# A hybrid encoder block on one core: the DMA queue written out in the plan's order, two gates by turns behind the rewriting of the input, and other durations in the planner

## The chip, the cores and the metric

The kernel runs on one core of one Trainium2 chip. The metric is the device time of one execution in microseconds. A core has TensorE (PE in the profile, its weight loads PEld), VectorE (DVE), ScalarE (ACT), GpSimd (POOL) and SyncE (SP), which here only issues DMAs. Each engine runs its own list of instructions in order; semaphores tie the lists together.

## The reference, cut to what matters

One layer of an encoder block over 512 positions of 1024 channels, float32:

```
h = rms_norm(x); p = h @ w_in        # q|k|v of a delta net, z, decays, q|k|v of attention, gates A and B
A: conv+silu on q,k,v, l2 norms, chunked gated delta rule in both directions
   (per chunk of 64 a unit lower triangular system is solved), gated norm, @ w_dn_out
B: three groups of 8 heads, windows with dilation 1, 4, 16 (keys by residue class),
   q and k normed, ALiBi, the groups weighted by their softmax denominators, @ w_attn_out
x = x + (sigmoid(gA)*yA + sigmoid(gB)*yB) @ w_o
x = x + (silu(conv(gate)) * conv(up)) @ w_ffn_down,  gate|up = rms_norm(x) @ w_ffn_up
```

## The kernel before, in words

Every dense product is made from three float32r matmuls (`mm3`, lines 317 to 320): operands are split into a high part and a rest, and high times high, high times rest and rest times high are added up in PSUM. Weights come from DRAM in blocks by class `Stream`: `load` (line 59) issues the DMA of a block into one of three buffers `wst`; `fetch` (line 69) has ScalarE write the high part `whi` (line 80) and GpSimd or VectorE the rest `wlo` (line 82); `block` hands out a block and fetches three further ones, each with two more loaded behind it.

The order of the dense work is the list `SEQ` (line 39): K (with the sum of squares of x beside it), AB (the delta net's decay and beta inputs, 32 columns), Q, then twelve attention units U (a head pair of one group each, `att_dense`, eight blocks of 384 columns), with V, Z and the sixteen gates between them, then YA, YB and WO and the feed-forward part. The units of groups 1 and 2, and all gates after unit 3, work on the input in residue-class order. So between unit 3 and the next gate the split input `hh`, `hl` is written anew: `by_classes` and `by_class` (lines 291 to 313) load x once more, scale it (line 304), let ScalarE write the high part (line 309) and VectorE the rest (line 311), for eight slices of 128 channels.

Beside the dense stream run generators: `chain` (delta net: decays, norms, gram matrices, the solve, the scan of eight chunks), `norms` and `queue` (attention: `att_norms` with the Newton iteration of `newton` at lines 257 to 262 and the transposes at 682 and 684, then `att_softmax`), and `combine` for each of four head pairs, which sends statistics through DRAM, makes weights, reads them back as broadcast tiles `alb` (line 850) and multiplies the group outputs with them (line 852). The solve is 31 steps of two VectorE operations (lines 957 and 960) on `xi`; its result goes to DRAM twice (`dx`, lines 964 and 965, the second transposed by VectorE, line 963) and comes back by twelve DMAs in other layouts (lines 973 and 976).

Where their instructions stand among the dense ones is decided by class `Driver` when the program is written: it keeps a clock `now`, advances it by each dense step (0.695 us, or 0.53 us in a unit), charges every VectorE, ScalarE and GpSimd operation a duration (`V`, `S`, `G`), and resumes a generator when its time is due. A generator that yields a number waits so long: LOAD for a DMA, TRIP for a way through DRAM and back, LATE before TensorE uses something, PACE between steps of the solve. `Slots` and `room` keep count of buffers by the planned time of their release. The line that fixes which engines keep that order is

```
ctx.enter_context(tc.manual_schedule(engines={PE, Activation, DVE, Pool}))      # names shortened
```

SP isn't in it: its DMAs are put in order by the framework's own scheduler. `drv.finish(dn)` ends the chain before the last LAST gates, and `post` (the gated norm) runs beside those.

Of the kernel before, what the change touches and what calls it, by code (L numbers as in the profile page):

```python
# [20 lines left out]
T = 512  # L21
# [12 lines left out]

UNITS = [(0, p) for p in range(4)] + [(g, p) for p in range(4) for g in (1, 2)]
GATES = [(n, d) for n in ("GA", "GB") for d in range(8)]
LAST = 4

SEQ = ([("K", 0), ("AB", 0)] + [("Q", i) for i in range(4)] + [("U", 0)] + [("V", i) for i in range(4)]
       + [("Z", 0), ("U", 1), ("Z", 1), ("Z", 2), ("U", 2), ("Z", 3), GATES[0], ("U", 3)]  # L40
       + [x for i in range(4, 12) for x in (GATES[i - 3], ("U", i))] + GATES[9:]
       + [(n, d) for n in ("YA", "YB") for d in range(8)] + [("WO", d) for d in range(8)])

LOAD, TRIP, LATE = 5.0, 9.0, 1.0
PACE = 2.0
TAIL, WARM = 2, 11
NBLK = {"K": 8, "AB": 1, "Q": 2, "V": 2, "U": 8, "Z": 2, "YB": 1, "GB": 2, "YA": 1, "GA": 2, "WO": 2}
WIDTH = {"AB": 256, "U": 384}


# [69 lines left out]
class Driver:  # L120
# [16 lines left out]
        self.end = max(self.end, t)  # L137

    def V(self, n, k=1):
        self.charge("V", k * (0.09 + n * 1.15e-3))  # L140
        return self.nc.vector

    def S(self, n, k=1):
# [72 lines left out]
def hybrid(tc, A, out):  # L216
# [3 lines left out]
    def pool(stack, name, side=None, **kw):  # L220
        kw.setdefault("reuse_waits", "tile")
        if side:
            kw["side"] = side
        return stack.enter_context(tc.tile_pool(name=name, bufs=1, **kw))

    ctx.enter_context(tc.manual_schedule(engines={mybir.EngineType.PE, mybir.EngineType.Activation, mybir.EngineType.DVE,
                                                   mybir.EngineType.Pool}))
    drv = Driver(nc)
    V, S, G, pe = drv.V, drv.S, drv.G, drv.pe
    cp = pool(ctx, "cp")  # L230
# [23 lines left out]
    def newton(y, x, tmp, scale, bias):  # L254
# [4 lines left out]
        for _ in range(3):  # L259
# [8 lines left out]
    ones = cp.tile([128, 128], F32, name="ones")  # L268
    nc.gpsimd.memset(ones, 1.0)
    ws = Stream(drv, nc, wp, A["wa"], [WIDTH.get(n, 512) for n, _ in SEQ for _ in range(NBLK[n])], 3, 6, "a",  # L270
                {b for b, n in enumerate(n for n, _ in SEQ for _ in range(NBLK[n])) if n in ("U", "Q", "V", "Z", "GA", "GB")})
    wt = Tiles(ws, 4)


# [14 lines left out]
    used = []  # L289

    def by_classes():
        xs = []
        for k in range(KD):
            while len(xs) < min(k + 2, KD):
                yield from drv.room(T2)
                xs.append(t2("xk"))
                nc.sync.dma_start(xs[-1], A["xt"][:, len(xs) - 1, :])
            while k not in used:
                yield 0.3
            drv.add(by_class(k, xs[k]))  # L300

    def by_class(k, xk):
        w = vec[:, V_N1 + k:V_N1 + k + 1]
        V(512).scalar_tensor_tensor(xk, xk, w, rstd, op0=ALU.mult, op1=ALU.mult)
        yield
        parts(k, "r")
        xo = xk.rearrange("p (j r) -> p r j", r=4)
        ho, lo = (a.rearrange("p (r j) -> p r j", r=4) for a in (hh[k], hl[k]))
        S(1024).activation(ho, xo, AF.Copy)
        yield  # L310
        V(900).tensor_tensor(lo, xo, ho.bitcast(F32), ALU.subtract)  # L311
        drv.give(T2)
        flags["class", k] = True

    acc = cp.tile([128, T], F32, name="acc", tag="rstd")

# [6 lines left out]
    warm = small_ps()  # L323
    for _ in range(WARM):
        nc.tensor.matmul(warm[:, 0:128], ones, ones, start=True, stop=True)
    for k in range(KD):
        xk = t2("xk")
        nc.sync.dma_start(xk, A["xt"][:, k, :])
        ws.fetch(min(k + 2, 8))
        hidden(k, xk)  # L330
        sq = acc if k == 0 else t2("sq")
        nc.scalar.activation(sq, xk, AF.Square)
        if k:
            nc.gpsimd.tensor_tensor(acc, acc, sq, ALU.add)
        if k == 5:
            nc.vector.tensor_copy(con[:, 0:1], xk[:, 0:1])
            nc.sync.dma_start(con, A["con"])
        wh, wl = ws.block(0)
        for m in range(4):
            c = slice(m * 128, m * 128 + 128)  # L340
            mm3(kps[m], wh[:, c], wl[:, c], hh[k], hl[k], k == 0, k == KD - 1)
# [47 lines left out]
            drv.dense(0.695)  # L389
        return ps  # L390

    def h_dense(ps=None, classes=False):
        def part(k):
            if classes:
                drv.until(lambda: ("class", k) in flags)
            return hh[k]
        return cm_dense(part, lambda k: hl[k], KD, ps)

    def conv(src, w0, scale_bc):

# [254 lines left out]
    def att_norms(u, qk):  # L655
# [9 lines left out]
        for i in range(2):  # L665
            V(512).tensor_reduce(ss[:, 0, i * 8:i * 8 + 8], sqs[i].rearrange("p i (a c) -> p i a c", c=64),  # L666
                                 axis=AX.X, op=ALU.add)
        drv.give(T2, 2)
        newton(ss[:, 1], ss[:, 0], ss[:, 2], 1.0 / 64, EPS)
        qk4 = qk.rearrange("p i (a c) -> p i a c", c=64)  # L670
        V(1024).tensor_tensor(qk4, qk4, ss[:, 1].rearrange("p (i a) -> p i a", a=4)[:, :, :, None]
                              .to_broadcast([128, 4, 4, 64]), ALU.mult)
# [127 lines left out]
    def combine(p):  # L800
# [4 lines left out]
        for g in (1, 2):  # L805
            nc.sync.dma_start(dst[p, g - 1].rearrange("(i r) c -> i (r c)", r=4),
                              stat[:, g].rearrange("p r h c -> p (r h c)"))
        for g in (1, 2):
            nc.sync.dma_start(nstat[:, g].rearrange("p a h c -> p a (h c)"),
                              dst[p, g - 1].rearrange("(a p) c -> p a c", p=128))  # L810
        V(16).tensor_copy(nstat[:, 0], stat[:, 0])
        yield TRIP
        al = ap_.tile([128, 3, 4, 2], F32, name="al")
        nM = ap_.tile([128, 4, 2], F32, name="nM")
        tt = ap_.tile([128, 4, 2], F32, name="tt")
# [26 lines left out]
        nc.sync.dma_start(o, dog[p])  # L842
        yield LOAD
        drv.give(T2)
        for g in range(3):
            yield from drv.room(T2)
            e = t2("alb")
            for h in range(2):
                c = (g * 2 + h) * 4
                nc.sync.dma_start(e[HALF[h]], daw[p, c:c + 4].rearrange("a t -> (a t)")[None].to_broadcast([64, T]))  # L850
            yield LOAD
            V(512).tensor_tensor(ogs[g, p], ogs[g, p], e, ALU.mult)
            drv.give(T2)
            if g:
                V(512).tensor_tensor(o, o, ogs[g, p], ALU.add)
# [22 lines left out]
    def gram(s):  # L878
        yield from drv.room(PG, 2)
        pg_ = [small_ps(), small_ps()]  # L880
        for p in range(4):
            for e, hf in DIAG:
                R = HALF[e]
                nc.tensor.matmul(pg_[e][HALF[hf], p * 128:p * 128 + 128], kq[R, p, s, 0, hf, :], kq[R, p, s, :, hf, :],
                                 start=True, stop=True)
        pe(2.4)
        for f in range(2):
            dg = dgs[s, f]
            for e in range(2):
                g4 = pg_[e].rearrange("p (q c t) -> p c q t", c=2, t=64)  # L890
                o4 = lambda x: x[:, f, s].rearrange("p (q e) t -> p e q t", e=2)[:, e]
                V(256).tensor_tensor(o4(cx), g4[:, 0], par(dg, e), ALU.mult)
                V(256).tensor_tensor(o4(qd), g4[:, 1], par(dg, e), ALU.mult)
                if f:
                    drv.give(PG)
            yield
            G(512).tensor_tensor(cx[:, f, s], cx[:, f, s], bc64(hs(AA, f, s)), ALU.mult)
            c = C_QKM + f * 64
            G(512).tensor_tensor(qd[:, f, s], qd[:, f, s], con[:, None, c:c + 64].to_broadcast([128, 8, 64]), ALU.mult)

    dgs = {}

# [13 lines left out]
    def chain():  # L916
# [30 lines left out]
        for f in range(2):  # L947
            for a in range(2):
                for b in range(2):
                    P = slice(a * 64 + b * 32, a * 64 + b * 32 + 32)  # L950
                    nc.sync.dma_start(du(dl)[f, a, b], cx[P, f].rearrange("p s h t -> p (s h) t")[:, :, b * 32:b * 32 + 32])
        nc.sync.dma_start(lt, dl)
        yield 2 * LOAD
        for j in range(31):
            n = 31 - j
            t4 = tmp[:, 0:2 * n * (j + 1)].rearrange("p (b i c) -> p b i c", b=2, i=n)
# [2 lines left out]
            xr = xi[:, :, j + 1:32, 0:j + 1]  # L959
            V(2 * n * (j + 1)).tensor_tensor(xr, xr, t4, ALU.add)  # L960
            yield PACE
        xt_ = n3.tile([128, 2, 32, 32], F32, name="xt_", tag="lt")
        V(2048).tensor_copy(xt_, xi.rearrange("p b i j -> p b j i"))
        nc.sync.dma_start(dx[0], xi)
        nc.sync.dma_start(dx[1], xt_)
        aux = n1.tile([128, 2, 32, 32], F32, name="aux", tag="tmp")
        cxf = cx.rearrange("p f s h t -> p f (s h) t")
        for f in range(2):
# [234 lines left out]
    def dense(n, i):  # L1203
        if n == "U":
            att_unit(i)
        elif n == "V":
            begin(qkv_tile("V", 8 + i, vT[:, i], h_dense(), PD))
        elif n == "Z":
            begin(out_gate(i, h_dense()))
        else:  # L1210
            begin(gate(GATES.index((n, i)), h_dense(None, classes), classes))

    for n, i in order[:-LAST]:
        dense(n, i)
# [100 lines left out]
    x1 = xp.tile([128, KD, T], F32, name="x1")  # L1315
    h2h = [cp.tile([128, T], F32R, name="h2h", tag=f"hh{k}") for k in range(KD)]
    h2l = [cp.tile([128, T], F32R, name="h2l", tag=f"hl{k}") for k in range(KD)]
    acc2 = xp.tile([128, T], F32, name="acc2")
    ws2 = Stream(drv, nc, xp, A["wb"], [1024] * A["wb"].shape[0], 2, 4, "b")
    for d in range(KD):  # L1320
        xk = t2("xk2")
        nc.sync.dma_start(xk, A["xt"][:, d, :])
        ps = cm_dense(lambda k: mh[:, k], lambda k: ml[:, k], KD)
        V(512).tensor_tensor(x1[:, d], ps, xk, ALU.add)
        drv.give(PD)
# [66 lines left out]
def prep(inputs):  # L1392
# [19 lines left out]
    for n, i in SEQ:  # L1412
# [4 lines left out]
        elif n == "U":  # L1417
            g, p = UNITS[i]
            c = slice((g * 8 + 2 * p) * 64, (g * 8 + 2 * p + 2) * 64)
            new = list(np.concatenate([kp(wq)[:, :, c], kp(wk)[:, :, c], kp(wv)[:, :, c]], axis=2))  # L1420
        else:
            new = rows(src[n][i])
        assert len(new) == NBLK[n]
# [61 lines left out]
```

## Time and profile before

| | |
|---|---|
| median of 3 runs | 1076.61 us (1075.24 to 1076.73) |
| the profiled execution | 1076.4 us, its span 1074.5 us |
| PE busy | 1008.2 us (94%), 6653 matmuls |
| DVE / ACT / POOL busy | 668.5 (62%) / 434.4 (40%) / 245.7 us (23%) |
| chain that ended last | PE 71%, DVE 14%, issue 5%, ACT 3%, DMA 3%, POOL 3% |
| DMA | 114.61 MB, queue of SP 33.1% of 16 engines' span |

A line of a timeline reads: start in us, duration in us, engine, line, operation, output and inputs, count, and in brackets the idle time of the engine before it and what ended it. "PEclk" is the TensorE clock that was granted, as a share of full speed.

### The profile page before, as it was taken

What the parts mean: (1) busy time and instruction counts of PE and PEld (TensorE: products, weight loads), DVE (VectorE), ACT (ScalarE), POOL (GpSimd) and SP (SyncE); (2) the same over time, 40 slices, a digit from 0 to 9 for tenths busy, and PEclk for the clock granted to TensorE, in tenths of its full rate; (3) what the DMA queues carried; (4) which work ended last, traced back from release to release, by engine and by line L of the source; (5) the groups of instructions that cost most, each with busy time, mean ns of one, the idle gap of its engine ahead of it and who ended that gap; (6) DMA issues with size and microseconds to landing.
All of it is one profiled execution on the core that took longest, in us unless ns stands there. A gap on an engine that the chain in (4) does not pass through costs nothing.

```text
span 1074.5 us, 17109 instructions
## 1 busy us (share of the span) xinstructions
PE 1008.2 (94%) x6653; PEld 841.3 (78%) x6653; DVE 668.5 (62%) x1139; ACT 434.4 (40%) x857; POOL 245.7 (23%) x229
## 2 busy tenths in 40 slices
PE   9879898987999959989999999999999999999998
PEld 7569686975999848878788787878888888888886
DVE  5384976569677634664765767667777225777621
ACT  5246445646555424334236423434334113433410
POOL 3234464523444512343443000200000000000000
PEclk9889998998999969999999999999999999999999
DMA  5222233542233482222364445412222322222331
GB/s 188 81 73 74 81 106 110 123 150 84 75 99 98 152 139 65 81 81 71 96 187 149 166 137 195 149 47 91 98 98 84 130 81 79 98 99 79 109 126 40
DMA packets 80288, 114.61 MB, mean 107 GB/s; under 512 B 32624, under 2 KB 45264, under 8 KB 79824
## 3 DMA queue, kind: packets, MB, share of 16 engines
q1 hardware_dynamic: 77328, 108.29, 33.1%
q10 hardware_dynamic: 2880, 5.24, 1.3%
q8 instruction: 52, 0.85, 0.3%
q14 instruction: 28, 0.23, 0.1%
HBM read 101.04 MB, written 12.47 MB: 106 GB/s over the span
## 4 chain that ended last, share of the span: by engine, by line
PE 71%; DVE 14%; issue 5%; ACT 3%; DMA 3%; POOL 3%; SPq 1%; POOLq 0%; ACTq 0%; DVEq 0%
PE dps L318 21%; PE dps L319 20%; PE dps L320 20%; POOL wlo L82 2%; PE gps L719 2%; PE gps L770 1%; DMA wst<-in_wa 1%; PE gps L754 1%; DMA xk<-in_xt 1%; DVE ass L666 1%; DVE wlo L82 1%; DVE cy L408 1%; PE gps L1060 1%; ACT whi L80 1%; DVE ass L260 1%
## 5 line engine op out<-in xcount | busy, mean ns | idle before, releaser
L82 POOL TENSOR_TENSOR wlo<-wst,whi 128x384 fp32r<-128x384 f32 (+1 forms) x152 | 178.9, 1186 | 322.8 <-ACT whi L80 286.8
L80 ACT ACTIVATE whi<-wst 128x384 fp32r<-128x384 f32 (+2 forms) x259 | 174.1, 690 | 129.3 <-PE dps L319 66.2
L318 PE MATMUL dps<-h2h,whi 128*128 128x512 f32 x352 | 139.2, 395 | 0.0
L320 PE MATMUL dps<-h2h,wlo 128*128 128x512 f32 x352 | 139.0, 395 | 0.0
L319 PE MATMUL dps<-h2l,whi 128*128 128x512 f32 x352 | 139.0, 395 | 0.0
L82 DVE TENSOR_TENSOR wlo<-wst,whi 128x1024 fp32r<-128x1024 f32 (+2 forms) x107 | 115.2, 1086 | 18.8 <-ACT whi L80 18.8
L406 ACT ACTIVATE cy<-pre,vec 128x512 f32<-128x512 f32 x56 | 40.6, 725 | 146.0 <-DVE pre L403 145.9
L318 PE MATMUL dps<-whi,hr 128*128 128x384 f32 x256 | 93.1, 364 | 0.0
L319 PE MATMUL dps<-wlo,hr 128*128 128x384 f32 x256 | 87.8, 343 | 0.0
L320 PE MATMUL dps<-whi,lr 128*128 128x384 f32 x256 | 87.8, 343 | 0.0
L319 PEld LDWEIGHTS dps<-h2l,whi 128*128 128x128 f32 x352 | 66.1, 188 | 16.0
L318 PEld LDWEIGHTS dps<-h2h,whi 128*128 128x128 f32 x352 | 66.1, 188 | 16.0
L320 PEld LDWEIGHTS dps<-h2h,wlo 128*128 128x128 f32 x352 | 66.1, 188 | 15.9
L318 PE MATMUL dps<-ah,whi 128*128 128x512 f32 x176 | 69.8, 397 | 0.0
L319 PE MATMUL dps<-al__7594,whi 128*128 128x512 f32 x176 | 69.6, 396 | 0.0
L320 PE MATMUL dps<-ah,wlo 128*128 128x512 f32 x176 | 69.2, 393 | 0.0
L408 DVE SCALAR_TENSOR_TENSOR cy<-pre,vec,cy 128x511 f32<-128x511 f32 x56 | 44.8, 799 | 36.2 <-ACT cy L406 36.1
L742 ACT ACTIVATE sb<-sb,stat 128x128 f32<-128x128 f32 (+1 forms) x96 | 40.8, 426 | 53.2 <-DVE stat L731 53.0
L1385 DVE TENSOR_TENSOR x<-x,dps 128x512 f32<-128x512 f32 x16 | 11.0, 686 | 78.8 <-PE dps L320 78.8
L318 PE MATMUL dps<-hh,whi 128*128 128x512 f32 x128 | 55.0, 430 | 2.1 <-ACT hh L286 2.1
L318 PE MATMUL dps<-hr,whi 128*128 128x512 f32 x120 | 50.4, 420 | 4.3 <-DVE v L646 2.4
L319 PE MATMUL dps<-lr,whi 128*128 128x512 f32 x120 | 48.9, 408 | 5.9 <-DVE lr L311 5.9
(298 smaller groups left out, 2112.8 us busy)
## 6 DMA issues: line engine op xcount, KB each, us to landing
wst<-in_wb SPq DMA_DIRECT2D x66, 512.0 KB, 3.2
wst<-in_wa SPq DMA_DIRECT2D x96, 256.0 KB, 2.7
wst<-in_wa SPq DMA_DIRECT2D x96, 192.0 KB, 2.3
xk<-in_xt SPq DMA_DIRECT2D x24, 256.0 KB, 3.3
dgt<-gt ACTq DMA_DIRECT2D x16, 256.0 KB, 2.0
alb<-daw SPq DMA_DIRECT2D x24, 128.0 KB, 3.2
dg<-dgd SPq DMA_DIRECT2D x16, 128.0 KB, 2.9
ga<-dgt SPq DMA_DIRECT2D x8, 256.0 KB, 3.8
```

The source lines that it names most:

```text
L80: self.drv.S(w).activation(hi[:, :w], st[:, :w], AF.Copy)
L82: eng(w).tensor_tensor(lo[:, :w], st[:, :w], hi[:, :w].bitcast(F32), ALU.subtract)
L260: V(n).tensor_mul(tmp, x, y)
L318: nc.tensor.matmul(ps, wh, xh, start=first, stop=False)
L319: nc.tensor.matmul(ps, wh, xl, start=False, stop=False)
L320: nc.tensor.matmul(ps, wl, xh, start=False, stop=last)
L406: S(512).activation(y, pre, AF.Copy, scale=w[1])
L408: V(512).scalar_tensor_tensor(y[:, 1:], pre[:, :-1], w[0], y[:, 1:], op0=ALU.mult, op1=ALU.add)
L666: V(512).tensor_reduce(ss[:, 0, i * 8:i * 8 + 8], sqs[i].rearrange("p i (a c) -> p i a c", c=64), axis=AX.X, op=ALU.add)
L719: nc.tensor.matmul(pss[h][:, t], qT[H, x, i:i + 128], kT[H, y, i:i + w], start=(n == 0), stop=(n == 2))
L742: S(w, 1.15).activation(sbs[b, h][:, t], sbs[b, h][:, t], AF.Exp, bias=st[:, 0:1], accum_out=st[:, 1:2])
L1385: V(512).tensor_tensor(x1[:, d], x1[:, d], ps, ALU.add)
```

## The change

SP's DMAs too stand in the order in which the program is written; so loads are written earlier (x in `load_x`, two `alb` tiles at once), and generators yield between writing to DRAM and reading back. Gates 1 and 2 become one item GP after the rewriting, whose blocks alternate, and one gate goes to the end, so that units 4 and 5, and 10 and 11, are neighbours. While slices 3 to 7 are rewritten, the solve pauses. The rewriting gets precedence (delays of -2). PACE is 1 for 2, LATE 1.5 for 1, TRIP 8 for 9, LAST 5 for 4. A VectorE operation is charged at least 0.28 us.

```diff
-LAST = 4
+LAST = 5
...
-       + [x for i in range(4, 12) for x in (GATES[i - 3], ("U", i))] + GATES[9:]
+       + [("GP", 1), ("U", 4), ("U", 5)] + [x for i in range(6, 11) for x in (GATES[i - 3], ("U", i))] + [("U", 11)]
+       + GATES[8:]
...
-LOAD, TRIP, LATE = 5.0, 9.0, 1.0
-PACE = 2.0
+LOAD, TRIP, LATE = 5.0, 8.0, 1.5
+PACE = 1.0
...
     def V(self, n, k=1):
-        self.charge("V", k * (0.09 + n * 1.15e-3))
+        self.charge("V", k * max(0.28, 0.08 + n * 1.2e-3))
...
-    ctx.enter_context(tc.manual_schedule(engines={mybir.EngineType.PE, mybir.EngineType.Activation, mybir.EngineType.DVE,
-                                                   mybir.EngineType.Pool}))
+    ctx.enter_context(tc.manual_schedule())
...
-            drv.add(by_class(k, xs[k]))
+            drv.add(by_class(k, xr[k]), -2.0)
...
         flags["class", k] = True
+        if k == 2:
+            flags["rewrite"] = True
+        if k == KD - 1:
+            del flags["rewrite"]
...
+    def load_x(upto):
+        while len(xs) < min(upto, KD):
+            xs.append(t2("xk"))
+            nc.sync.dma_start(xs[-1], A["xt"][:, len(xs) - 1, :])
+
+    load_x(1)
+    ws.load(1)
+    load_x(2)
     for k in range(KD):
-        xk = t2("xk")
-        nc.sync.dma_start(xk, A["xt"][:, k, :])
+        xk = xs[k]
         ws.fetch(min(k + 2, 8))
+        load_x(k + 3)
...
+        if k == KD - 1:
+            ws.fetch(9)
...
+    def pair_dense():
+        drv.need(PD, 2)
+        ps = [dense_ps(), dense_ps()]
+        for k0 in (0, 4):
+            for i in range(2):
+                wh, wl = ws.block()
+                for k in range(k0, k0 + 4):
+                    drv.until(lambda: ("class", k) in flags)
+                    c = slice((k - k0) * 128, (k - k0) * 128 + 128)
+                    mm3(ps[i], wh[:, c], wl[:, c], hh[k], hl[k], k == 0, k == KD - 1)
+                    drv.dense(0.695)
+        return ps
...
         drv.give(T2, 2)
+        yield
         newton(ss[:, 1], ss[:, 0], ss[:, 2], 1.0 / 64, EPS)
+        yield
...
+        yield LOAD
         for g in (1, 2):
             nc.sync.dma_start(nstat[:, g].rearrange("p a h c -> p a (h c)"),
...
-        yield TRIP
+        yield LOAD
...
+        es = []
         for g in range(3):
-            yield from drv.room(T2)
-            e = t2("alb")
...
+            while len(es) < min(g + 2, 3):
+                yield from drv.room(T2)
+                e = t2("alb")
...
+                es.append((e, drv.now + LOAD))
+            yield max(0.0, es[g][1] - drv.now)
...
             yield PACE
+            while "rewrite" in flags:
+                yield 0.5
         xt_ = n3.tile([128, 2, 32, 32], F32, name="xt_", tag="lt")
+        nc.sync.dma_start(dx[0], xi)
         V(2048).tensor_copy(xt_, xi.rearrange("p b i j -> p b j i"))
-        nc.sync.dma_start(dx[0], xi)
+        yield
         nc.sync.dma_start(dx[1], xt_)
+        yield TRIP
```

The two GpSimd masks after a gram matrix become a generator of their own, and the loads of x beside WO go one step further ahead, by `load_x`.

## Rows read from the trace of the kernel before

**Rows 1.** Busy time by stretch: stretch, its length, engines (instructions), PEclk, DMA share, GB/s.
```profile
0.00:600.00 600.00, 539.64 (x4641) 465.31 (x4641) 388.25 (x770) 275.10 (x640) 235.90 (x222) 0.95 0.37 107
600.00:1050.00 450.00, 447.69 (x1924) 359.51 (x1925) 277.49 (x367) 159.28 (x218) 9.79 (x7) 1.00 0.33 110
```
**Rows 2.** Who PE waited for: us in total, times, longest.
```profile
PE gps L682 <- DVE qk L671: 21.8, 4, 12.5
PE dps L319 <- DVE lr L311: 5.9, 2, 5.5
PE gps L505 <- DVE pre L499: 4.7, 1, 4.7
...
PE dps L318 <- DVE v L646: 2.4, 1, 2.4
...
PE gps L320 <- DVE wlo L82: 2.3, 1, 2.3
```
**Rows 3.** Busy time in the K steps and behind five of the waits; columns as in rows 1.
```profile
7.00:33.30 26.30, 24.93 (x99) 19.45 (x99) 13.82 (x16) 13.56 (x24) 10.81 (x9) 0.94 0.48 148
...
36.84:46.00 9.16, 9.16 (x30) 4.48 (x31) 0.62 (x2) 1.26 (x2) 2.51 (x2) 0.67 0.45 143
59.64:67.00 7.36, 7.36 (x28) 5.87 (x29) 4.34 (x10) 3.06 (x10) 1.28 (x1) 0.54 0.02 3
178.70:183.30 4.60, 4.58 (x16) 4.01 (x17) 2.51 (x4) 3.23 (x6) 1.07 (x2) 0.56 0.17 61
...
264.90:271.40 6.50, 6.11 (x17) 5.00 (x18) 1.94 (x3) 1.61 (x2) 1.07 (x2) 0.50 0.11 42
...
397.35:404.80 7.45, 7.45 (x105) 6.62 (x107) 3.27 (x5) 2.28 (x4) 1.01 (x1) 0.51 0.12 18
```
**Rows 4.** Timeline of PE: two of the four waits at line 682.
```profile
178.72 1.11 PE L682 MATMUL gps<-con,qk 128*128 128x128 f32 x4 [5.25 <-DVE qk L671]
220.21 1.06 PE L682 MATMUL gps<-con,qk 128*128 128x128 f32 x4 [2.64 <-DVE qk L671]
```
**Rows 5.** Timeline of DVE: one Newton iteration beside GpSimd, one without, the last rewritten slice.
```profile
170.36 0.59 DVE L257 TENSOR_SCALAR ass<-ass 128x16 f32<-128x16 f32 x1
...
177.43 1.23 DVE L671 TENSOR_TENSOR qk<-qk,ass 128x1024 f32<-128x1024 f32 x1
...
260.32 0.17 DVE L257 TENSOR_SCALAR ass<-ass 128x16 f32<-128x16 f32 x1
...
262.63 1.23 DVE L671 TENSOR_TENSOR qk<-qk,ass 128x1024 f32<-128x1024 f32 x1
...
265.80 1.07 DVE L311 TENSOR_TENSOR lr<-xk,hr 128x512 fp32r<-128x512 f32 x1
```
**Rows 6.** Timeline of POOL: one of six operations in a row, 169 to 176 us.
```profile
173.10 1.05 POOL L897 TENSOR_TENSOR cx<-cx,sm 128x512 f32<-128x512 f32 x1
```
**Rows 7.** Line 957, a solve step's first operation: ns min/median/max, first and last start.
```profile
L957 DVE TENSOR_TENSOR tmp<-lt,xi x31: 224/608/1626, 230.7 to 365.2; 128x62 f32<-128x62 f32 x2, 128x120 f32<-128x120 f32 x2, 128x174 f32<-128x174 f32 x2, 128x224 f32<-128x224 f32 x2
```
**Rows 8.** Timeline of SP's queue behind the solve.
```profile
370.13 0.41 SPq L965 DMA_DIRECT2D dx<-xt__3767  x1
371.82 0.34 SPq L976 DMA_DIRECT2D aux<-dx  x1
377.15 2.15 SPq L973 DMA_DIRECT2D cx<-dx  x4
...
385.55 1.21 SPq L66 DMA_DIRECT2D wst<-in_wa  x2
386.82 1.09 SPq L850 DMA_DIRECT2D alb<-daw  x2
```
**Rows 9.** Who waited for whom from 366 to 400 us.
```profile
ACT whi L80 <- DMA wst<-in_wa: 19.4, 3, 13.0
DVE og L852 <- DMA alb<-daw: 14.4, 1, 14.4
```
**Rows 10.** DMA issues by line: count, KB each, us from issue to landing.
```profile
alb<-daw SPq DMA_DIRECT2D x24, 128.0 KB, 3.2
```

More of the change, by code (lines that the diff above doesn't have):

```diff
@@ L36 @@
 GATES = [(n, d) for n in ("GA", "GB") for d in range(8)]
-LAST = 4
+LAST = 5
 SEQ = ([("K", 0), ("AB", 0)] + [("Q", i) for i in range(4)] + [("U", 0)] + [("V", i) for i in range(4)]
        + [("Z", 0), ("U", 1), ("Z", 1), ("Z", 2), ("U", 2), ("Z", 3), GATES[0], ("U", 3)]
-       + [x for i in range(4, 12) for x in (GATES[i - 3], ("U", i))] + GATES[9:]
+       + [("GP", 1), ("U", 4), ("U", 5)] + [x for i in range(6, 11) for x in (GATES[i - 3], ("U", i))] + [("U", 11)]
+       + GATES[8:]
        + [(n, d) for n in ("YA", "YB") for d in range(8)] + [("WO", d) for d in range(8)])
-LOAD, TRIP, LATE = 5.0, 9.0, 1.0
-PACE = 2.0
+LOAD, TRIP, LATE = 5.0, 8.0, 1.5
+PACE = 1.0
 TAIL, WARM = 2, 11
-NBLK = {"K": 8, "AB": 1, "Q": 2, "V": 2, "U": 8, "Z": 2, "YB": 1, "GB": 2, "YA": 1, "GA": 2, "WO": 2}
+NBLK = {"K": 8, "AB": 1, "Q": 2, "V": 2, "U": 8, "Z": 2, "YB": 1, "GB": 2, "GP": 4, "YA": 1, "GA": 2, "WO": 2}
 WIDTH = {"AB": 256, "U": 384}
@@ L270, in hybrid @@
     ws = Stream(drv, nc, wp, A["wa"], [WIDTH.get(n, 512) for n, _ in SEQ for _ in range(NBLK[n])], 3, 6, "a",
-                {b for b, n in enumerate(n for n, _ in SEQ for _ in range(NBLK[n])) if n in ("U", "Q", "V", "Z", "GA", "GB")})
+                {b for b, n in enumerate(n for n, _ in SEQ for _ in range(NBLK[n])) if n in ("U", "Q", "V", "Z", "GA", "GB", "GP")})
     wt = Tiles(ws, 4)
@@ L291, in by_classes @@
     def by_classes():
-        xs = []
+        xr = []
         for k in range(KD):
-            while len(xs) < min(k + 2, KD):
+            while len(xr) < min(k + 2, KD):
                 yield from drv.room(T2)
-                xs.append(t2("xk"))
-                nc.sync.dma_start(xs[-1], A["xt"][:, len(xs) - 1, :])
+                xr.append(t2("xk"))
+                nc.sync.dma_start(xr[-1], A["xt"][:, len(xr) - 1, :])
             while k not in used:
                 yield 0.3
-            drv.add(by_class(k, xs[k]))
+            drv.add(by_class(k, xr[k]), -2.0)
     def by_class(k, xk):
@@ L304, in by_class @@
         V(512).scalar_tensor_tensor(xk, xk, w, rstd, op0=ALU.mult, op1=ALU.mult)
-        yield
+        yield -2.0
         parts(k, "r")
@@ L309, in by_class @@
         S(1024).activation(ho, xo, AF.Copy)
-        yield
+        yield -2.0
         V(900).tensor_tensor(lo, xo, ho.bitcast(F32), ALU.subtract)
@@ L325, in hybrid @@
         nc.tensor.matmul(warm[:, 0:128], ones, ones, start=True, stop=True)
+    xs = []
+    def load_x(upto):
[5 more added lines that the diff above has]
+    load_x(2)
     for k in range(KD):
-        xk = t2("xk")
-        nc.sync.dma_start(xk, A["xt"][:, k, :])
+        xk = xs[k]
         ws.fetch(min(k + 2, 8))
+        load_x(k + 3)
         hidden(k, xk)
@@ L390, in cm_dense, with h_dense @@
         return ps
[L392 to L397, printed above, removed]
+    def h_dense(ps=None):
+        return cm_dense(lambda k: hh[k], lambda k: hl[k], KD, ps)
+    def pair_dense():
[10 more added lines that the diff above has]
+        return ps
     def conv(src, w0, scale_bc):
@@ L844, in combine @@
         drv.give(T2)
+        es = []
         for g in range(3):
-            yield from drv.room(T2)
-            e = t2("alb")
[L848 to L852, printed above, removed]
+            while len(es) < min(g + 2, 3):
+                yield from drv.room(T2)
+                e = t2("alb")
+                for h in range(2):
+                    c = (len(es) * 2 + h) * 4
+                    nc.sync.dma_start(e[HALF[h]], daw[p, c:c + 4].rearrange("a t -> (a t)")[None].to_broadcast([64, T]))
+                es.append((e, drv.now + LOAD))
+            yield max(0.0, es[g][1] - drv.now)
+            V(512).tensor_tensor(ogs[g, p], ogs[g, p], es[g][0], ALU.mult)
             drv.give(T2)
@@ L896, in gram, with masks @@
             yield
-            G(512).tensor_tensor(cx[:, f, s], cx[:, f, s], bc64(hs(AA, f, s)), ALU.mult)
-            c = C_QKM + f * 64
-            G(512).tensor_tensor(qd[:, f, s], qd[:, f, s], con[:, None, c:c + 64].to_broadcast([128, 8, 64]), ALU.mult)
+            drv.add(masks(f, s))
+    def masks(f, s):
+        G(512).tensor_tensor(cx[:, f, s], cx[:, f, s], bc64(hs(AA, f, s)), ALU.mult)
+        c = C_QKM + f * 64
+        G(512).tensor_tensor(qd[:, f, s], qd[:, f, s], con[:, None, c:c + 64].to_broadcast([128, 8, 64]), ALU.mult)
+        yield
     dgs = {}
@@ L951, in chain @@
                     nc.sync.dma_start(du(dl)[f, a, b], cx[P, f].rearrange("p s h t -> p (s h) t")[:, :, b * 32:b * 32 + 32])
+        yield LOAD
         nc.sync.dma_start(lt, dl)
-        yield 2 * LOAD
+        yield LOAD
         for j in range(31):
@@ L961, in chain @@
             yield PACE
+            while "rewrite" in flags:
+                yield 0.5
         xt_ = n3.tile([128, 2, 32, 32], F32, name="xt_", tag="lt")
+        nc.sync.dma_start(dx[0], xi)
         V(2048).tensor_copy(xt_, xi.rearrange("p b i j -> p b j i"))
-        nc.sync.dma_start(dx[0], xi)
+        yield
         nc.sync.dma_start(dx[1], xt_)
+        yield TRIP
         aux = n1.tile([128, 2, 32, 32], F32, name="aux", tag="tmp")
@@ L1207, in dense @@
             begin(qkv_tile("V", 8 + i, vT[:, i], h_dense(), PD))
+        elif n == "GP":
+            for j, ps in enumerate(pair_dense()):
+                begin(gate(i + j, ps, True))
         elif n == "Z":
@@ L1210, in dense @@
         else:
-            begin(gate(GATES.index((n, i)), h_dense(None, classes), classes))
+            begin(gate(GATES.index((n, i)), h_dense(), classes))
     for n, i in order[:-LAST]:
@@ L1317, in hybrid @@
     h2l = [cp.tile([128, T], F32R, name="h2l", tag=f"hl{k}") for k in range(KD)]
+    xs.clear()
     acc2 = xp.tile([128, T], F32, name="acc2")
@@ L1320, in hybrid @@
     for d in range(KD):
-        xk = t2("xk2")
-        nc.sync.dma_start(xk, A["xt"][:, d, :])
+        load_x(d + 2)
+        xk = xs[d]
         ps = cm_dense(lambda k: mh[:, k], lambda k: ml[:, k], KD)
@@ L1420, in prep @@
             new = list(np.concatenate([kp(wq)[:, :, c], kp(wk)[:, :, c], kp(wv)[:, :, c]], axis=2))
+        elif n == "GP":
+            a, b = (rows(src[m][j]) for m, j in GATES[i:i + 2])
+            new = [a[0], b[0], a[1], b[1]]
         else:
```

## The prediction, on record before the changed kernel ran

> **What bounds the kernel now.** I read first the busy time in two long stretches [rows 1]. From 600 to 1050 us TensorE is busy for 447.69 of 450 us at full clock: 1924 matmuls, 0.2327 us each. Nothing in the diff shortens a matmul there, so all that can be won lies before 600 us. There TensorE is busy for 539.64 of 600 us, at a mean clock of 0.95. So 60 us are idle, and about 0.05 x 540 = 27 us go to the lower clock.
>
> Next comes the list of what TensorE waited for [rows 2]; the reader is to see that nearly all of its long waits end on VectorE, and that one line, the transposes behind the attention norms, holds 21.8 us in four waits, one of them 12.5 us. Third, the stretches behind those waits [rows 3]: behind each the granted clock is lower (0.50 to 0.67 as a mean: mostly the lower of its two levels, 1.2 GHz). A wait here costs its length and then (1 - clock) x busy. Fourth, SP's queue at the longest wait [rows 8, 9].
>
> **The change part by part.** Durations are those of the profiled execution, 1076.4 us in all (span 1074.5), 0.2 us below the median of the runs shown.
>
> *K steps and AB.* The split of the AB block (its rest on VectorE) now stands ahead of the last K products, not behind the Newton iteration that waits for them. The 2.3 us wait [rows 2] goes, and with it the slow stretch: 0.33 x 9.16 = 3.0 us [rows 3]. The eight K steps take 26.3 us, of which 96 matmuls x 0.2327 = 22.3 are work; x two slices ahead could give back up to 4.0 us, but weights and x still share one queue in turns and four buffers, so I take 1. Sum 6.3, bounds 0 and 9.3.
>
> *Decays (line 505).* 4.7 us, and 0.46 x 7.36 = 3.4 us of clock behind it [rows 2, 3]. Sixteen operations of 64 elements were charged 0.09 + 64 x 0.00115 = 0.164 us and are now charged 0.28: 16 x 0.116 = 1.9 us, and LATE adds 0.5. So 2.4 us more dense work stands ahead of the waiting matmuls. The rest of the wait stays, and I leave the clock with it. Gain 2.4, bounds -1 (placed later than needed, the chain's successors come later) and 8.1.
>
> *Attention norms (line 682).* Without the 12.5 us wait the three others make 21.8 - 12.5 = 9.3 us, 5.25 and 2.64 among them [rows 2, 4], hence a third of 1.4. Eleven operations of 16 elements go from 0.108 to 0.28 us in the plan: 1.9, with LATE 2.4 us. Each wait shrinks by at most that: 1.4 + 2.4 + 2.4 = 6.2. Clock behind the 5.25 us: 0.44 x 4.58 = 2.0, not counted. Bounds: all of it, 11.3, and -3, if the later transposes hold back the softmax and so the next unit.
>
> That charge is where a rule weighs against the change. The same eleven operations took 262.63 - 260.32 = 2.3 us in one place and 177.43 - 170.36 = 7.1 us in another [rows 5], where GpSimd ran operations of about 1 us one behind the other [rows 6]. The charge of 11 x 0.28 = 3.1 us covers the first and not the second. The Trainium skill, page SBUF — State Buffer, section "Who interferes with whom", says that a VectorE operation with two SBUF inputs and a GpSimd operation that reads SBUF exclude each other for the whole of the one that began first. The stretched operations agree with it; by it a charge per operation can't be right for both places, which is the second rival below.
>
> *Rewriting (line 311).* The gate behind unit 3 waited 5.9 us for the rest of slices 6 and 7, then 0.5 x 6.11 = 3.1 us went to the clock [rows 2, 3]. The last slice was written at 265.80 us, behind the norms of unit 3 (to 263.9) and solve steps [rows 5]. Now both stand back: the solve pauses, the rewriting has precedence, and TensorE has two gates' products on slices 0 to 3 (8 x 0.695 = 5.6 us, before 2.8) before it needs slice 4. That is 2.8 us of cover more, and VectorE freed of 3.5 us of norms (Newton and the scaling, 260.32 to 263.9). 6.3 us exceed 5.9. I take 7.5 of 9.0, since unit 3's norms now come later; bounds 0 and 9.
>
> *Behind the solve.* SP issued the second write at 370.13 and the first read back at 371.82, then stood until 377.15 for the write to land; the twelve reads took until 385.55, and only then came weights and `alb` [rows 8]. ScalarE waited 13.0 us for weights, VectorE 14.4 us for `alb` with the norms of a unit queued behind that multiplication [rows 9]; TensorE's waits of 2.4 and 12.46 us followed, then 0.49 x 7.45 = 3.7 us of clock: 18.6 us [rows 2, 3]. In plan order eight planned microseconds lie between write and reads, in which weights and `alb` are issued. The standing (5.3 us) goes; the issuing of twelve (8.4 us) stays, with weights behind it, but six blocks of 12 x 0.175 = 2.1 us are ahead (0.175: 0.2327 x 384/512, an estimate), 12.6 us of cover against 8.4 plus a landing. I take 12, since something of `alb` may still fall behind the twelve; bounds 0 and 18.6. If the cover is gone, the wait is back.
>
> *What it adds.* A queue written in plan order stops at every DMA whose data isn't there; weights are behind it then. No row shows that order. Bounds: a little below nothing, since the other stalls before 600 us could also shrink (say 2 us), and on the other side one or two waits as behind the solve, 12.46 + 3.7 = 16.2 us each. I take half of one, 8. PACE 1: the solve took 136 us for 31 steps, 4.4 each [rows 7]; one microsecond less each brings the scan some 25 us forward, but VectorE's work gets denser there. Units 4 and 5 as neighbours: the fourth PSUM bank of unit 4 waits for two gate evictions; with the denser VectorE 0.8 us. LAST, the masks, the three yields elsewhere and `load_x` beside WO: nothing; dense work with its weights ahead hides them, as the full stretch after 600 us shows [rows 1], and what they would cost without it is inside the 8 us.
>
> Sum: 6.3 + 2.4 + 6.2 + 7.5 + 12 - 8 - 0.8 = 25.6 us; 1076.4 - 25.6 = **1051 us**.
>
> **The rivals.**
> - *The wait behind the solve moves.* With PACE 1 the solve's end meets the combination of the first head pair elsewhere, and `alb` or weights again stand behind the twelve reads. For it: the 8.4 us are unchanged, and the plan charges SP nothing for issuing. Against: the standing before them is gone. No gain of 12: 1063 us.
> - *VectorE becomes the bound.* Where GpSimd splits weights beside the norms, eleven operations cost 7.1 us against 3.1 charged, and the denser solve takes VectorE's gaps. The 2.4 and 6.2 are lost, and a wait of 5.25 us comes twice more: 1051 + 8.6 + 10.5 = 1070 us. By the rule of the skill named above this comes wherever the two meet.
> - *Given back.* The order of the queue was good already, and the holes only wander: 1076 us, no change.
> - *Slower: each combination stalls.* `alb` lands 3.2 us after issue [rows 10] and is planned at LOAD = 5. If SP is over 1.8 us behind the plan at the issue, because a weight load ahead waits for GpSimd, VectorE stops at line 852 with the norms behind it. Before, one of four combinations did this, for 14.4 us; if the three others do too, each with 16.2 us: 1076.4 - 22.4 + 48.6 = 1103 us (no gain behind the solve). At half of that the whole gain is gone. Against it: twelve such multiplications, and only one waited, in a queue that also waits for GpSimd.
>
> **How the numbers follow.** The forecast 0.52 (its own range 1038 to 1060), the moved wait 0.20, VectorE 0.12, given back 0.06, slower 0.10. From 1035 to 1074 us about two in ten are left out: the last two cases and a small part below. A measurement here tells changes of over 0.2%, 2.2 us, from none. Faster: 0.52 + 0.20 + 0.11 = 0.83; same 0.06; slower 0.11.
>
> **What would show it.** Right: no wait of TensorE over 4 us between 30 and 600 us except perhaps near line 505; the clock at 1.00 where the rewriting ends and behind the solve; weights issued between the writes and the reads of `dx`; the solve over in about 110 us. Wrong: ScalarE waiting over 10 us for weights, VectorE over 5 us for `alb`, or a busy share of TensorE before 600 us no higher than now.

## The result, and the profile after

The changed kernel takes 1045.07 us (median; before, on the same chip, 1075.92): a ratio of 0.9718, 95% interval 0.9692 to 0.9745. That is 30.9 us less; 25.6 were forecast, 1051 us.

The page of the changed kernel: span, busy time, granted clock in 40 slices, the chain that ended last.

```profile
span 1043.2 us, 17128 instructions
...
PE 1001.0 (96%) x6653; PEld 838.3 (80%) x6653; DVE 676.1 (65%) x1139; ACT 433.3 (42%) x857; POOL 252.8 (24%) x229
...
PEclk9999989989999989999999999999999999999999
...
PE 67%; DVE 14%; issue 6%; ACT 5%; DMA 4%; POOL 2%; SPq 2%; POOLq 0%; ACTq 0%; DVEq 0%
```

Busy time by stretch, which answers to [rows 1], columns as there; the third line is the stretch from the end of unit 3 to the start of unit 4.

```profile
0.00:570.00 570.00, 537.11 (x4673) 466.77 (x4673) 401.05 (x783) 277.67 (x646) 243.19 (x222) 0.97 0.39 114
570.00:1020.00 450.00, 444.38 (x1897) 356.13 (x1898) 272.98 (x353) 155.67 (x212) 9.59 (x7) 1.00 0.32 108
...
235.90:258.00 22.10, 16.40 (x88) 12.66 (x89) 15.01 (x27) 15.28 (x32) 8.61 (x8) 0.92 0.19 58
```

TensorE idles for 33 of the first 570 us, where it idled for 60 of 600. By the mean clocks of the whole spans, 0.969 before and 0.982 after, the lower clock cost 0.031 x 1074.5 = 33 us and now costs 0.018 x 1043.2 = 19.

Who TensorE waited for, the longest of the list and the two that answer to [rows 2] (line 710 was 682, 311 kept its number):

```profile
PE dps L322 <- DVE z L1214: 5.1, 1, 5.1
PE gps L798 <- DVE pt L787: 4.4, 4, 1.7
PE dps L322 <- ACT v L677: 4.4, 1, 4.4
PE gps L782 <- ACT sb L770: 4.3, 2, 3.0
PE dps L322 <- DVE pre L429: 2.6, 1, 2.6
PE gps L531 <- DVE pre L525: 2.2, 1, 2.2
...
PE gps L710 <- DVE qk L699: 0.5, 1, 0.5
...
PE dps L323 <- DVE lr L311: 0.2, 1, 0.2
```

The 21.8 us behind the norms are 0.5, the 5.9 us behind the last slices 0.2, the 4.7 us of the decays 2.2, and the wait for the AB split is gone. In their place stand waits that were short or not there: 5.1 us of unit 1 for a PSUM bank (0.7 before), 4.3 us for exponentials (2.1 before), and 4.4 us for ScalarE's copies of unit 3 (none before), just where the rewriting is.

Where the lead arises can be read by landmarks that both programs have, from the starts and ends of their matmuls (us):

| | before | after | lead | of it in this stretch |
|---|---|---|---|---|
| unit 0 starts | 77.7 | 67.5 | 10.2 | 10.2 |
| unit 3 ends | 252.7 | 235.9 | 16.8 | 6.6 |
| unit 5 ends (gates 0 to 2 done in both) | 321.3 | 303.8 | 17.5 | 0.7 |
| unit 7 ends | 373.5 | 359.9 | 13.6 | -3.9 |
| YA starts | 607.1 | 571.7 | 35.4 | 21.8 |
| the norm of the feed-forward part starts | 702.0 | 671.1 | 30.9 | -4.5 |

SP's queue behind the solve, which answers to [rows 8]:

```profile
350.69 0.33 SPq L1002 DMA_DIRECT2D dx<-xi  x1
351.12 9.36 SPq L67 DMA_DIRECT2D wst<-in_wa  x3
360.57 0.35 SPq L869 DMA_DIRECT2D daw<-awT  x1
...
361.37 0.42 SPq L1005 DMA_DIRECT2D dx<-xt__3731  x1
361.89 1.73 SPq L67 DMA_DIRECT2D wst<-in_wa  x2
363.67 3.26 SPq L881 DMA_DIRECT2D alb<-daw  x4
...
367.61 1.46 SPq L1014 DMA_DIRECT2D cx<-dx  x2
...
379.14 2.11 SPq L67 DMA_DIRECT2D wst<-in_wa  x1
```

Weights and four of the six `alb` loads now go out between the write (361.37) and the reads (367.61). The twelve reads still hold the queue, for 11.5 us. And the second write itself is late: 10.7 us pass between the two writes, where 3.4 passed before. VectorE has the transposed copy ready at 357.7 us, and until 361.4 the write stands behind weights, whose buffers GpSimd is still reading (SP waits 8.2 us for that between the two writes), and behind the write of `daw`. GpSimd's subtraction in front of them took 3.46 us beside that copy of 2.35 us; the next one of the same size, without it, took 1.29 us.

Of the signs that the prediction gave of being right, three are missing: TensorE has two waits of over 4 us between 30 and 600 us (5.1 and 4.4), the clock is 0.92 in the stretch with the rewriting and 0.93 from 350 to 400 us, not 1.00, and the solve took 129 us, not 110. One of its signs of being wrong is there too: ScalarE waited 11.3 us for weights behind the twelve reads (until 383.3 us). TensorE had cover for it; from 360 to 400 us it waited 2.0 us for the reads themselves and 2.0 us for VectorE.

### The profile page after: what moved, and what is told of

The parts are those of the page before. It is cut to its first block, busy times and chain, and to the rows that moved or that the text cites. A ratio compares the mean times of both kernels' runs of the same rounds, so it can differ in the third digit from the quotient of the medians.

```text
span 1043.2 us, 17128 instructions
## 1 busy us (share of the span) xinstructions
PE 1001.0 (96%) x6653; PEld 838.3 (80%) x6653; DVE 676.1 (65%) x1139; ACT 433.3 (42%) x857; POOL 252.8 (24%) x229
## 4 chain that ended last, share of the span: by engine, by line
PE 67%; DVE 14%; issue 6%; ACT 5%; DMA 4%; POOL 2%; SPq 2%; POOLq 0%; ACTq 0%; DVEq 0%
PE dps L322 20%; PE dps L323 20%; PE dps L324 20%; DMA wst<-in_wa 3%; POOL wlo L83 2%; PE gps L747 1%; PE gps L798 1%; DVE wlo L83 1%; ACT sb L770 1%; DVE tmp L994 1%; ACT whi L81 1%; DVE ass L261 1%; PE gps L782 1%; DVE cy L434 1%; DVE ass L260 1%
## 5 line engine op out<-in xcount | busy, mean ns | idle before, releaser
L83 POOL TENSOR_TENSOR wlo<-wst,whi 128x384 fp32r<-128x384 f32 (+1 forms) x152 | 184.6, 1226 | 284.4 <-ACT whi L81 264.4
L83 DVE TENSOR_TENSOR wlo<-wst,whi 128x1024 fp32r<-128x1024 f32 (+2 forms) x107 | 117.6, 1106 | 20.9 <-ACT whi L81 20.8
L322 PE MATMUL dps<-whi,hh 128*128 128x384 f32 x128 | 46.7, 365 | 7.7 <-DVE z L1214 5.1
```

What stands on the lines that cost most here:

```text
L83: eng(w).tensor_tensor(lo[:, :w], st[:, :w], hi[:, :w].bitcast(F32), ALU.subtract)
L322: nc.tensor.matmul(ps, wh, xh, start=first, stop=False)
```

## The experiments

Each is the changed kernel or the kernel before with the edit shown, timed beside the kernel before. Differences in the last column are those of the ratios x 1075 us; the changed kernel is 0.9718 by that measure. A difference of two such ratios is known to 0.3 to 0.5% (3 to 5 us): the 4 us of a_no_pair can't be told from nothing, and the 4 us of a_sp_auto only just.

| | edit | us (median) | ratio, 95% interval | against changed or before |
|---|---|---|---|---|
| a_sp_auto | changed, SP by the framework | 1040.19 | 0.9679 (0.9662 to 0.9696) | -4 |
| b_sp_plan | before, SP in plan order | 1086.8 | 1.0107 (1.009 to 1.0124) | +12 |
| a_old_times | changed, old durations | 1060.22 | 0.9864 (0.9841 to 0.9887) | +16 |
| a_old_charge | changed, old VectorE charge | 1059.71 | 0.9851 (0.9808 to 0.9893) | +14 |
| a_dx_at_once | changed, no yield at dx | 1049.67 | 0.9765 (0.9751 to 0.978) | +5 |
| a_alb_dx | changed, that and alb singly | 1054.37 | 0.9812 (0.979 to 0.9833) | +10 |
| b_alb_dx | before, alb in twos, yield at dx | 1058.07 | 0.9856 (0.9824 to 0.9888) | -15 |
| a_no_pair | changed, gates singly, LAST 4 | 1047.86 | 0.9751 (0.9724 to 0.9779) | +4 |
| a_no_pause | changed, no pause, no precedence | 1032.64 | 0.9612 (0.9578 to 0.9647) | -11 |
| a_no_prec | changed, no precedence | 1056.1 | 0.983 (0.9795 to 0.9865) | +12 |
| a_pace2 | changed, PACE 2 | 1058.95 | 0.9862 (0.9827 to 0.9897) | +15 |
| a_best | changed, no pause, no precedence, SP by the framework | 1022.96 | 0.9522 (0.9489 to 0.9556) | -21 |

### The order of the queue, both ways

```diff
-    ctx.enter_context(tc.manual_schedule())                       # a_sp_auto; b_sp_plan is the reverse, in the kernel before
+    ctx.enter_context(tc.manual_schedule(engines={PE, Activation, DVE, Pool}))
```

> The changed kernel with SP's DMAs ordered by the framework again, all else as changed. Theory (plan order is what took the wait behind the solve away): that wait returns, ScalarE waits over 8 us for weights behind the read back of dx, 1045 + 10 to 18 = 1055 to 1063 us. Rival (the yields, durations and the order of units did it, the queue's order is worth nothing): 1042 to 1048 us and no such wait.

> The kernel before with one edit, SP's DMAs in program order. Theory (the order pays only with yields between a write to DRAM and its read back, as SP stands at the first read): 1066 to 1082 us, SP standing some 5 us or more at the first read of dx with weights behind it. Rival (the order alone brings most of the gain): below 1060 us.

Measured: a_sp_auto 4 us less than the changed kernel, b_sp_plan 12 us more than the kernel before. So the theory of the first is wrong, and its rival was only half right: the plan's order isn't worthless, it costs. In the second, SP stood at the first read as expected (5.2 us), but the time is above the range given for it. In a_sp_auto four `alb` loads go out at 363.89 us, ahead of nine of the twelve reads, with no help of the order. In b_sp_plan the old wait behind the solve grew (waits from 362 to 405 us; compare [rows 9]):

```profile
ACT whi L80 <- DMA wst<-in_wa: 21.5, 3, 16.5
DVE og L851 <- DMA alb<-daw: 17.7, 1, 17.7
...
PE gps L681 <- DVE qk L670: 17.4, 1, 17.4
```

This wait is the smaller part of the 12 us: from the end of unit 7 to the end of unit 8 the two kernels differ by 2.1 us (65.2 and 63.1), from the end of unit 11 to YA by 6.8 (55.0 and 48.2), where TensorE waited 6.2 us for VectorE in the gated norm (line 1253; 1.6 before).

What SP's queue waited for is changed by the order, here in the changed kernel:

```profile
SPq L869 <- DVE awT L867: 21.5, 3, 9.7
SPq L826 <- ACT og L802: 14.8, 4, 5.2
```

In plan order a small DMA whose data is late holds the weights behind it; with the framework's order (a_sp_auto) the queue waited 3.4 and 2.6 us at these two places. How much of that reaches TensorE isn't shown there. At one place it is: from YA to the norm of the feed-forward part the changed kernel takes 2.8 us more than a_sp_auto, and TensorE waits for weights there, which it doesn't in a_sp_auto:

```profile
PE dps L324 <- DVE wlo L83: 1.2, 1, 1.2
PE dps L322 <- ACT whi L81: 0.9, 1, 0.9
```

From YA to the start of the feed-forward matmuls the four kernels with the framework's order take 91.2 to 93.0 us, the ten in plan order 93.3 to 96.4.

### Behind the solve: the yield, and alb two at a time

```diff
         nc.sync.dma_start(dx[1], xt_)
-        yield TRIP                                  # a_dx_at_once
...
-            while len(es) < min(g + 2, 3):          # a_alb_dx: this too, as in the kernel before
+            yield from drv.room(T2)
...
+        yield TRIP                                  # b_alb_dx: both edits alone, in the kernel before
```

> The changed kernel without the yield of 8 us between the second write of dx and the reads. Theory (these 8 planned us let weights out ahead of the reads): SP stands 4 to 6 us at the first read, TensorE waits 6 to 15 us behind it, 1052 to 1060 us. Rival (plan order alone is enough, the weights are far enough ahead): 1042 to 1048 us.

> The changed kernel with the alb tiles loaded one at a time again and without the yield before the reads of dx; SP in plan order as changed. Theory (these two, not the order of the queue, put alb ahead of the twelve reads): the wait of the norms for VectorE and of VectorE for alb comes back with 8 to 17 us, 1055 to 1066 us. Rival (the shift of the solve against the combination did it): as without the yield alone, 1048 to 1052 us.

> The kernel before with two edits, alb two at a time and a yield of TRIP (9 us) before the reads of dx; SP's order left to the framework. Theory (these two suffice for the wait behind the solve): no wait of over 5 us for alb or weights there, 1075 - 10 to 18 = 1057 to 1065 us. Rival (only with the plan's order or the new durations): 1070 us or more.

Measured: +5, +10 and -15 us. The first lies between its two expectations, and so, just, does the second. TensorE waited twice for the reads themselves (3.3 and 3.2 us in a_dx_at_once, 3.4 and 3.3 in a_alb_dx; once, 2.0, in the changed kernel), in none of the three for weights. ScalarE's longest wait for weights grew from 11.3 us to 14.9 and 15.8. In a_alb_dx:

```profile
ACT whi L81 <- DMA wst<-in_wa: 16.7, 2, 15.8
...
PE gps L1026 <- DMA cx<-dx: 3.4, 1, 3.4
PE gps L1026 <- DMA aux<-dx: 3.3, 1, 3.3
```

The old stall of VectorE for `alb` didn't come back. The third run decides it: in the kernel before, with the framework's order of the queue, the two edits alone give 15 us. There all six `alb` loads stand ahead of the first read, and VectorE waits 3.2 us for them, not 14.4:

```profile
376.29 2.38 SPq L852 DMA_DIRECT2D alb<-daw  x4
...
382.58 1.09 SPq L852 DMA_DIRECT2D alb<-daw  x2
...
384.34 1.04 SPq L977 DMA_DIRECT2D cx<-dx  x2
```

### The durations

```diff
-        self.charge("V", k * max(0.28, 0.08 + n * 1.2e-3))
+        self.charge("V", k * (0.09 + n * 1.15e-3))             # a_old_charge; a_old_times has the next too
-LOAD, TRIP, LATE = 5.0, 8.0, 1.5
+LOAD, TRIP, LATE = 5.0, 9.0, 1.0
```

> The changed kernel with the old charge of VectorE, LATE 1.0 and TRIP 9. Theory (the durations put 2.4 us more work ahead of the transposes of the attention norms and of the decays' matmuls): waits of together 6 to 11 us there come back, 1045 + 6 to 12 = 1051 to 1057 us. Rival (durations only shuffle the waits): 1042 to 1048 us.

> The changed kernel with the old charge of VectorE alone, LATE 1.5 and TRIP 8 kept. Theory (the charge of 0.28 for small operations carries three quarters of what the durations brought, 1.9 of 2.4 us per place): 1052 to 1058 us, waits behind the norms and the decays back. Rival (LATE carries it): 1043 to 1049 us.

Measured: +16 and +14 us, a little above both theories (to 1057 and to 1058 us). The charge of VectorE carries it; LATE and TRIP add nothing to the time that can be told from it. The edit takes back the whole formula, in which an operation of 512 to 1024 elements differs by 0.02 to 0.04 us and one of 16 by 0.17, so that it is the small ones is likely; it wasn't tried alone. What TensorE waited for in a_old_charge:

```profile
PE dps L322 <- ACT v L677: 8.0, 2, 7.7
PE dps L322 <- DVE gt L1234: 6.7, 1, 6.7
PE gps L710 <- DVE qk L699: 5.2, 4, 2.1
PE gps L1305 <- DVE oo L1298: 5.1, 1, 5.1
PE gps L531 <- DVE pre L525: 5.1, 1, 5.1
```

The waits named in the forecast are there (lines 710 and 531, 10.3 us against 2.7), but as much comes at other places, where VectorE, and at line 677 ScalarE, came later than TensorE needed them.

### The rewriting: pair, pause, precedence

```diff
-       + [("GP", 1), ("U", 4), ("U", 5)] + ...                # a_no_pair: SEQ and LAST as before
-            while "rewrite" in flags:                          # a_no_pause: this and the next
-                yield 0.5
-            drv.add(by_class(k, xr[k]), -2.0)                  # a_no_prec: this, and both yields of -2.0
+            drv.add(by_class(k, xr[k]))
```

> The changed kernel with the gates one by one again between the units and LAST 4, the rest (pause and precedence of the rewriting too) as changed. Theory (two gates' products cover the rewriting): TensorE waits 3 to 6 us longer near line 311, with its clock down behind it, 1045 + 3 to 8 = 1048 to 1053 us. Rival (pause and precedence are enough, and a gate between units 4 and 5 helps the norms): 1040 to 1046 us.

> The changed kernel without the pause of the solve and without the precedence of the rewriting, the pair of gates kept. Theory (VectorE's order is what ended the wait for the last slices): the last slice comes 4 to 8 us later, 1045 + 3 to 8 = 1048 to 1053 us. Rival (the pair alone covers it): 1042 to 1047 us.

> The changed kernel without the precedence of the rewriting (delays of -2), the pause of the solve kept. Theory (precedence puts ScalarE's write of the next slice ahead of the unit's evictions before its data is there, and both engines wait for each other): TensorE's wait of 4.4 us at the first gate goes, the rewriting ends some 4 us sooner, 1033 to 1038 us. Rival (the pause is what costs, by the later solve and scan): 1042 to 1047 us.

Measured: +4, -11 and +12 us. The 4 us of a_no_pair are near its theory, but its wait near line 311 was 1.8 us against 0.2, less than the 3 to 6 expected. a_no_pause goes against its theory and its rival alike: pause and precedence together cost 11 us. Between the end of unit 3 and the start of unit 4 stand one gate (5.6 us) before and in a_no_pair, two (11.1 us) in the others. What is over them: before 15.2 - 5.6 = 9.6 us, changed 22.1 - 11.1 = 11.0, a_no_pair 17.0 - 5.6 = 11.4, a_no_pause 16.5 - 11.1 = 5.4, a_no_prec 14.9 - 11.1 = 3.8, a_best (below) 19.8 - 11.1 = 8.7. So the pair can cover part of the rewriting, but not with the precedence; one gate without the precedence was run only in the kernel before, so that it is the pair isn't shown. What the precedence does is seen in the changed kernel's timelines, first ScalarE, then VectorE:

```profile
229.70 1.13 ACT L309 ACTIVATE hr<-xk 128x512 fp32r<-128x512 f32 x1 [2.17 <-DVE xk L304]
...
235.94 1.11 ACT L309 ACTIVATE hr<-xk 128x512 fp32r<-128x512 f32 x1 [0.93 <-PE dps L324]
...
239.81 0.36 ACT L677 ACTIVATE v<-dps,rtok 64x128 f32<-64x128 f32 x1
240.20 1.13 ACT L309 ACTIVATE hr<-xk 128x512 fp32r<-128x512 f32 x1
```
```profile
230.86 1.10 DVE L311 TENSOR_TENSOR lr<-xk,hr 128x512 fp32r<-128x512 f32 x1 [1.26 <-ACT hr L309]
...
237.08 1.08 DVE L311 TENSOR_TENSOR lr<-xk,hr 128x512 fp32r<-128x512 f32 x1 [1.23 <-ACT hr L309]
...
241.36 1.09 DVE L311 TENSOR_TENSOR lr<-xk,hr 128x512 fp32r<-128x512 f32 x1 [1.58 <-ACT hr L309]
...
247.71 1.08 DVE L311 TENSOR_TENSOR lr<-xk,hr 128x512 fp32r<-128x512 f32 x1 [3.93 <-ACT hr L309]
```

A delay of -2 puts ScalarE's and VectorE's parts of a slice next to each other in both lists; each engine then stands until the other is done (ScalarE 2.17 us at 229.7, VectorE 1.26 just after), and the eviction of unit 3 (line 677), for which TensorE waits 4.4 us, is in the same list. Without precedence (a_no_prec) that wait is 0.9 us and the last slice is ready 8.5 us sooner (242.8 against 251.3 us).

Yet a_no_prec is slower in all, against its theory and against its rival too, for the solve also ended sooner (its last step starts at 340.1 against 350.4 us). Its lead over the changed kernel was lost later, from 7.9 us at the end of unit 7 to -8.2 at the end of unit 11; what TensorE waited for from 270 to 560 us:

```profile
PE gps L798 <- DVE pt L787: 6.0, 3, 2.9
PE gps L1051 <- DVE qt L1036: 4.3, 1, 4.3
PE gps L1101 <- DVE r L1093: 4.1, 3, 2.1
PE dps L322 <- DVE v L672: 3.9, 2, 3.4
PE gps L1101 <- POOL vs L1078: 2.0, 1, 2.0
```

a_no_prec and a_no_pause differ by the pause alone: without the precedence it costs 23 us. Why it leads to these waits isn't settled, and the precedence without the pause wasn't run. Without both, the last step of the solve starts at 328.1 us and 11 us are gained.

### PACE, and the best of these edits together

```diff
-PACE = 1.0
+PACE = 2.0                                                    # a_pace2
```

> The changed kernel with PACE 2. Theory (the solve is off the path, its pace moves only where the scan falls): solve some 25 us longer, 1043 to 1050 us. Rival (an earlier scan gives the dense work at the end something to cover it, and is a good part of the gain): over 1052 us, with TensorE idle before the last gates.

> The changed kernel without precedence and pause and with SP's DMAs ordered by the framework. Theory (the two costs of 12 and 5 us are of different places and add up): 1026 to 1031 us. Rival (the framework's order gains only where the rewriting is late): 1031 to 1035 us.

Measured: +15 us for PACE 2, as the rival said. The solve lasts to 372 us, 22 longer. Until the end of unit 11 that costs nothing (498.7 against 508.1 us); the price comes from there to YA, which starts at 583.2 against 571.7 us. More of the scan then stands among the last gates: 867 matmuls in this stretch against 539, at a clock of 0.94 against 1.00. First a_pace2, then the changed kernel, the longest waits of TensorE from 395 to 600 us:

```profile
PE gps L1030 <- ACT og L804: 3.6, 1, 3.6
PE gps L1101 <- DVE nM L845: 3.4, 1, 3.4
PE gps L1101 <- POOL vs L1078: 3.4, 1, 3.4
PE gps L1101 <- DVE r L1093: 3.0, 1, 3.0
```
```profile
PE dps L322 <- ACT oa L1315: 2.2, 1, 2.2
```

No other wait of the changed kernel there is over 0.5 us in all.

a_best, without pause, precedence and plan order of the queue, takes 1022.96 us, 21 less than the changed kernel where -11 and -4 together would give 15, and where up to 19 (1026 us) was expected; the 6 us between 21 and 15 are within the noise of these four ratios together. TensorE is busy for 97% of its span.

## Why the prediction was right, and where it wasn't

The sum was near because its errors cancel, and that is luck: one term of 7.5 us brought 0.7, and one that stood at nothing was worth 15. By its own steps:

- **K steps and AB, 6.3.** Right. a_old_times and a_old_charge have these edits with the old charge, and in both unit 0 starts at 71.9 us, 5.8 before the 77.7 of the kernel before. The AB wait and the slow clock behind it are gone.
- **Decays, 2.4.** The wait shrank by 2.5 us, as worked out. Of the clock, which was left out, some came too: unit 0 starts 4.4 us earlier with the new charge than with the old one.
- **Attention norms, 6.2.** The stretch from unit 0 to the end of unit 3 gained 6.6 us, but not by the charge alone: up to unit 3 the waits at this line are 0.5 us with the new charge and 3.7 with the old one in an otherwise changed kernel, where two of those before were 5.25 and 2.64 [rows 4]. The new yields around the Newton iteration, costed at nothing, may be the rest; they weren't tried alone. And new waits (5.1 and 4.3 us) came. The rival drawn from GpSimd's operations had its condition but not its price: the eleven operations still took 2.3 to 5.4 us from first to last (up to 7.0 before) against 3.1 charged, and 0.5 us of waiting was left. The rule that it leans on speaks of operations with two inputs; two of the six stretched ones before, the first shown in [rows 5] among them, have one.
- **Rewriting, 7.5.** Wrong: the stretch to the end of unit 5 gained 0.7 us. "VectorE freed" was not the point; by precedence ScalarE's evictions were put behind slices that were not ready, and the pause held back the solve and the scan behind it. Without precedence, with the pair of gates, 3.8 to 8.7 us stand over the gates, not 9.6.
- **Behind the solve, 12.** The size was right (10 us in one direction, 15 in the other), the lever wrong: "in plan order eight planned microseconds lie between write and reads" is the work of the yield and of the two loads at once, and it works with the framework's order as well.
- **What the queue's order adds, -8.** The sign was right: 12 us in the kernel before, 4 in the changed one. The stretch from YA to the norm of the feed-forward part lost 4.5 us, of which 2.8 come back in a_sp_auto. The stretch from unit 5 to 7 lost 3.9, but it takes 56.1 us in the changed kernel and 56.2 in a_sp_auto, so that isn't the queue's order.
- **PACE, costed at nothing but 0.8 for the denser VectorE.** The largest miss: with PACE 2 the changed kernel takes 15 us more. The solve was off the path, but it decides how much of the scan is left for the last gates, where its dependent steps had too little dense work beside them. The forecast of 110 us for the solve was too short as well (129 us, for the pause; 107 without).

Of the rivals, the bound by VectorE didn't happen. The moved wait did in part: weights stood behind the twelve reads, but TensorE had cover for them. The slower one had its place right in part: the queue does stand at late data of the combinations (21.5 us for `awT`), but VectorE waited only 2.1 us for `alb`.

## What to carry to other kernels

Separate in a plan what changes the distance between a write and its read from what changes the order of a queue: here the first gave 10 to 15 us and the second took 4 to 12. Charge small operations what the trace shows, since an undercharge of 0.17 us, many times over, moves later waits. And when one list order holds the whole kernel, an edit that wins at its place (8.5 us at the rewriting, by taking the precedence out) can lose more later; undo each part alone and time the whole.

## What had not been expected of the hardware

The twelve reads of `dx`, 128 KB each, held SP's queue for 8.4 us before and 11.5 us in the changed kernel, 0.7 and 1.0 us each on average, while loads of weights of 192 or 256 KB shortly ahead of them took 0.33 to 0.45 us to issue. Most of the packets moved meanwhile are under 512 B (12599 of 13497 from 366 to 390 us before); that the short rows are the reason wasn't tested.
